# Weights-stationary product of a two-block transformer kernel: three 256-column matmuls a chunk in place of one of 512 and one of 256

## Chip, cores and metric

The kernel runs on one core of a Trainium2 chip. The metric is the device time of one execution in microseconds; lower is better. Three runs of the kernel before gave 3282.68, 3284.78 and 3285.42 us, so its time is the median, 3284.78 us.

## What is computed

Two transformer blocks over 256 tokens of 2048 features, all in float32. The lines that the change touches compute products of a weight matrix with the normed tokens, where the result is wanted with features on the partitions and tokens along the free axis:

```
proj = jnp.einsum('bsd,de->bse', h, w_in[l])            # block 1: q and k of two attentions
u = jax.nn.relu(jnp.einsum('bsd,df->bsf', h2, w_up[l])) # block 1: up projection, then u * u
proj = xn @ w_in[l]                                     # block 2: the mixers' projections
qry = jnp.einsum('td,dhk->thk', xt, w_query)            # block 2: PEER queries
hid = jax.nn.gelu(jnp.einsum('pd,phkd->phk', xb, u_tab[eb]), approximate=False)
y = jnp.einsum('phk,phkd->pd', gate * hid, v_tab[eb])
```

The last two lines are computed for all 16384 experts: `peer_u` holds them in 128 blocks of 128, and gates that are zero leave out the experts that were not chosen.

## The kernel before, in words

Every large product is made in two parts a factor: a float32 number is split into `hi` (rounded to float32r) and `lo` (the rest, also float32r), and of the four partial products the three largest are added up: hi·hi, hi·lo and lo·hi. The tokens are split once for each product stage into `XT`, two tiles of [128, 8, 2, 256], where the third axis is (hi, lo) and the last the 256 tokens. The weights come from HBM in pieces of [128, 2048], in two halves of [128, 1024] (`load`, L90), and each half is split as it arrives: ScalarE copies it to `hi` (L103), VectorE subtracts to give `lo` (L104).

There are two kinds of large product. In the first (`xpart`, L165 to L167, and `product`, L1184 to L1186) the tokens are stationary in TensorE and the weights move through in three matmuls of 512 columns. In the second, `wstat` (L117 to L130), the weights are stationary: for each of 16 chunks of 128 input features (8 to a half) the `hi` weights are loaded and all 512 columns of `XT` (hi and lo tokens) move through, into the full 512 columns of a PSUM bank (L125); then the `lo` weights are loaded and the 256 `hi` token columns move through, into the first half of that bank (L127). At the end the result is the sum of the two halves of the bank.

`wstat` is called 272 times, so 272 × 16 = 4352 pairs of matmuls: 64 times for the up projection (FFN), 128 times for `peer_u`, 16 times for the PEER queries and 64 times for the q, k and mixer projections (16 in each of `w1_qkf`, `w1_qka`, `w2_b`, `w2_fq`). Behind each call the two halves are added: ScalarE copies the second half to SBUF, VectorE adds the first half to it, and the rest of the work follows. These adds stand in `evac_w` (L285 and L286, then the scaling of L287), in the FFN (L516 and L517, then relu and square in L518), in the PEER queries (L1101 and L1102) and in the `peer_u` loop (L1151 and L1152, then the gelu in L1154 and L1156).

The order of the work on each engine is that of the program, with the split of the weights and the reading of results ahead (`tc.high_priority`), and a scheduler places the instructions of small background generators (attention, delta rule, HGRN2, top-k) between the large matmuls; `tick` moves them on after every half piece. In the `peer_u` loop the gate squares (`gates`, L1117) put two or four matmuls of 256 columns with their own stationary tiles between two `wstat` blocks. PSUM has four banks for results (`acc`) and four for small work (`misc`).

Of the kernel before, what the change touches and what calls it, by code (L numbers as in the profile page):

```python
# [21 lines left out]
OP = mybir.AluOpType  # L22
# [14 lines left out]
def build(tc, I, out):  # L37
# [27 lines left out]
    # ---- background work: generators that go on by a step after every half piece of weights, so that  # L65
# [42 lines left out]
    def split_to(hi, lo, src, scale=None):  # L108
        """hi, lo: float32r halves of src (times a per-partition scale)."""
        if scale is None:  # L110
            ins = S.activation(hi, src, AF.Copy)
            V.tensor_tensor(out=lo, in0=src, in1=hi.bitcast(F32), op=OP.subtract)  # L112
        else:
            ins = S.activation(hi, src, AF.Copy, scale=scale)
            V.scalar_tensor_tensor(lo, src, scale, hi.bitcast(F32), op0=OP.mult, op1=OP.subtract)  # L115
        return ins

    def wstat(src, X):
        """[128 features, 256 tokens] = W^T X; the two halves of the result's columns add up."""
        ps = acc()  # L120
        for s, (hi, lo) in enumerate(split(src)):
            for j in range(8):
                w = slice(j * 128, (j + 1) * 128)
                x = X[s][:, j]
                PE.matmul(ps, lhsT=hi[:, w], rhs=x.rearrange("p a t -> p (a t)"),  # L125
                          start=(s == 0 and j == 0), stop=False, skip_group_check=True)
                PE.matmul(ps[:, :T], lhsT=lo[:, w], rhs=x[:, 0], start=False,  # L127
                          stop=(s == 1 and j == 7), skip_group_check=True)
# [3 lines left out]
    def small_proj(name, n, X, r, pool, y, tag="evh"):  # L132
        """y [128 tokens, 2, n] = r * (X^T W) for a W of n columns, both of its parts stationary together"""
# [24 lines left out]
    def xpart(ps, part, X, k0, tt, first, last):  # L158
        """ps [128 tokens, 512 features] += X^T W over the two k-chunks of half a piece"""
# [9 lines left out]
    def xstat(srcs, X):  # L169
        """two banks [128 tokens, 512 features] = X^T W over the k-chunks of the pieces."""  # L170
# [9 lines left out]
    def out_proj(name, X, each):  # L180
        """X^T W in two k-halves of two feature blocks at a time: the second heads are needed late;
        each(nb, tt, ps) takes a result, and the very last pieces end with the first tokens first"""
# [25 lines left out]
    # matrix products that keep the tensor engine's clock up until the first data are there  # L208
# [36 lines left out]
    def rsqrt(dst, src, n, mul):  # L245
        """dst = (src * mul + eps) ** -0.5 for [128, n]"""
# [25 lines left out]
    def bcast(r, b, pool):  # L272
        """b [128, 256]: every partition holds r of the 256 tokens"""
# [7 lines left out]
    def evac_w(ps, dst, rB, pool):  # L281
        """dst = (first half + second half of the columns) * rB"""
        with tc.high_priority():
            t = pool.tile([128, T], F32, name="ev", bufs=3)
            ins = S.activation(t, ps[:, T:], AF.Copy)  # L285
            V.tensor_tensor(out=t, in0=ps[:, :T], in1=t, op=OP.add)  # L286
            V.tensor_tensor(out=dst, in0=t, in1=rB, op=OP.mult)  # L287
# [10 lines left out]
    def head_norm_t(o, dst, g, pool, h0, nh, z=None, ready=None):  # L298
        """dst[:, h] (hi, lo) = transpose of rmsnorm over the last axis of o[:, tt, h] (times z), times g"""
# [26 lines left out]
    # ================= block 1 =================  # L326
# [36 lines left out]
    # forgetting attention  # L363
# [81 lines left out]
    # stick-breaking attention  # L445
# [56 lines left out]
    # feed-forward in quarters of 2048 hidden features; the norm's scale is squared by relu^2  # L502
# [8 lines left out]
    def ffn_up(qr):  # L511
        hid[qr] = [act_tile(F32R), act_tile(F32R)]
        for f in range(16):
            ps = wstat(I["w1_up"][qr * 16 + f], XT)
            t = up.tile([128, T], F32, name="up_t", bufs=3)
            S.activation(t, ps[:, T:], AF.Copy)  # L516
            V.tensor_tensor(out=t, in0=ps[:, :T], in1=t, op=OP.add)  # L517
            V.scalar_tensor_tensor(t, t, 0.0, t, op0=OP.max, op1=OP.mult)  # L518
# [35 lines left out]
    # x = rmsnorm(x, g_final); the next norm's scale is that of x * g_final times both  # L554
# [12 lines left out]
    # ================= block 2: mixers =================  # L567
# [80 lines left out]
    def gdn_rest(j, ys):  # L648
        # l2 norms
# [14 lines left out]
        # beta * v, token layout  # L664
# [10 lines left out]
        # decays: L[t, s] and its transpose per tile, and from tile 0 to tile 1  # L675
# [50 lines left out]
        # Tm = (I - L)^-1 and its transpose U, by doubling  # L726
# [36 lines left out]
        # u = Tm (beta v - beta G u_prev), o = a u  # L763
# [128 lines left out]
    # four heads at a time, so that the activation tables of sigmoid, ln and exp change seldom  # L892
# [55 lines left out]
    # ================= block 2: PEER =================  # L948
# [27 lines left out]
    # queries, scores and the two rounds of top 16  # L976
# [30 lines left out]
    # A pair (i, j) of ranks can be among the 16 largest sums only if (i + 1) (j + 1) <= 16: all the pairs (i', j')  # L1007
    # with i' <= i and j' <= j come before it. So rows 0, 1 keep 16 columns, rows 2, 3 keep 8, rows 4..7 keep 4
    # and rows 8..15 keep one, in the order of the whole square.
    CANDS = ((0, 0, 2, 16), (32, 2, 2, 8), (48, 4, 4, 4), (64, 8, 8, 1))  # L1010

    def topk():
# [17 lines left out]
        # ranks of a pair: i the largest of p >> 4, (p >> 3) - 2, (p >> 2) - 8, p - 56, and j from the row's start  # L1030
# [19 lines left out]
        # gates  # L1050
# [9 lines left out]
        # chosen rows and columns of the expert square, slots on the partitions  # L1060
# [295 lines left out]
```

## Time and profile before

| what | value |
|---|---|
| median of three runs | 3284.78 us |
| lowest and highest run | 3282.68, 3285.42 us |
| span of the profiled execution | 3282.4 us |
| TensorE busy (PE) | 99% |
| weight loads busy (PEld) | 84% |
| VectorE, ScalarE busy | 67%, 52% |
| HBM traffic | 176 GB/s mean |

The page gives no time of the profiled execution apart from its span; the lowest run is 0.3 us above that span and the median 2.4 us. A matmul's recorded duration goes on past the start of the next matmul, because matmuls are pipelined, so the share of PE does not say how fast the columns go through; distances between starts do.

### The profile page before, as it was taken

Reading aid. Unit: us, or ns where it says so; the run is one execution under the profiler, and the core shown is the slowest. Engines: PE = TensorE matmul, PEld = TensorE weight load, DVE = VectorE, ACT = ScalarE, POOL = GpSimd, SP = SyncE. Lnnn points to the kernel's source line nnn. Section 1 sums busy time; section 2 is a strip of 40 time slices with the busy share of each in tenths; the row PEclk is TensorE's granted clock in tenths of the full one; section 3 lists DMA queues with packets and bytes.
Section 4 is the critical chain, followed back from the end, with each engine's and each line's share of the span. In section 5 each row is a group of like instructions: output and inputs, shape, how many; then the busy total and the mean of one; then the engine's idle time right before and its main releaser. Section 6 shows DMA issues by size and latency. Waiting matters only on the chain.

```text
span 3282.4 us, 45440 instructions
## 1 busy us (share of the span) xinstructions
PE 3254.2 (99%) x16980; PEld 2755.9 (84%) x16980; DVE 2191.2 (67%) x3659; ACT 1698.5 (52%) x2613; POOL 26.0 (1%) x40
## 2 busy tenths in 40 slices
PE   9999999999999999999999999999999999999998
PEld 7888888888888888888878888888888888888886
DVE  4556666555555686477669978888889655555554
ACT  5447554444443565555544456666555544444444
POOL 0000000000000000000000000000000000000000
PEclk9999999999999999999999999999999999999999
DMA  6454555555556543353455555555555655555654
GB/s 222 147 166 157 186 183 186 190 191 188 192 187 194 187 133 116 115 168 129 145 165 174 175 179 178 177 179 180 177 178 178 206 192 191 192 190 191 216 192 162
DMA packets 162415, 578.79 MB, mean 176 GB/s; under 512 B 19088, under 2 KB 20880, under 8 KB 161808
## 3 DMA queue, kind: packets, MB, share of 16 engines
q1 hardware_dynamic: 156384, 565.36, 52.6%
q10 hardware_dynamic: 5808, 10.52, 0.9%
q8 instruction: 133, 2.18, 0.3%
q14 instruction: 90, 0.74, 0.1%
HBM read 571.61 MB, written 4.19 MB: 175 GB/s over the span
## 4 chain that ended last, share of the span: by engine, by line
PE 92%; DVE 6%; ACT 1%; DMA 1%; issue 1%; POOL 0%; SPq 0%; DVEq 0%; POOLq 0%; ACTq 0%
PE acc L125 27%; PE acc L127 14%; PE acc L167 7%; PE acc L166 7%; PE acc L165 7%; PE acc L1186 7%; PE acc L1185 7%; PE acc L1184 7%; DVE lo L104 2%; PE misc L1117 1%; PE misc L873 1%; PE misc L758 1%; PE misc L750 1%; ACT hi L103 0%; PE misc L855 0%
## 5 line engine op out<-in xcount | busy, mean ns | idle before, releaser
L104 DVE TENSOR_TENSOR lo<-raw,hi 128x1024 fp32r<-128x1024 f32 x987 | 1206.6, 1223 | 867.5 <-ACT hi L103 523.4
L103 ACT ACTIVATE hi<-raw 128x1024 fp32r<-128x1024 f32 x1010 | 1070.4, 1060 | 1331.3 <-PE acc L166 368.6
L125 PE MATMUL acc<-xt,hi 128*128 128x512 f32 x4352 | 1554.8, 399 | 0.2 <-ACT hi L103 0.2
L127 PE MATMUL acc<-xt,lo 128*128 128x256 f32 x4168 | 1173.0, 281 | 1.4 <-DVE lo L104 1.3
L125 PEld LDWEIGHTS acc<-xt,hi 128*128 128x128 f32 x4352 | 819.2, 188 | 193.4 <-issue 2.3
L127 PEld LDWEIGHTS acc<-xt,lo 128*128 128x128 f32 x4168 | 782.9, 188 | 4.2 <-DVE lo L104 3.0
L1186 PE MATMUL acc<-lo,xt 128*128 128x512 f32 x1024 | 401.7, 393 | 1.2 <-DVE lo L104 1.2
L1185 PE MATMUL acc<-hi,xt 128*128 128x512 f32 x1024 | 401.7, 392 | 0.0
L1184 PE MATMUL acc<-hi,xt 128*128 128x512 f32 x1024 | 398.4, 389 | 0.0
L1184 PEld LDWEIGHTS acc<-hi,xt 128*128 128x128 f32 x1024 | 192.2, 188 | 43.6 <-DVE ut L1152 0.2
L1185 PEld LDWEIGHTS acc<-hi,xt 128*128 128x128 f32 x1024 | 192.3, 188 | 43.1 <-DVE xt L112 0.2
L1186 PEld LDWEIGHTS acc<-lo,xt 128*128 128x128 f32 x1024 | 192.3, 188 | 42.4 <-DVE lo L104 2.9
L167 PE MATMUL acc<-lo,act 128*128 128x512 f32 x512 | 199.5, 390 | 0.0
L166 PE MATMUL acc<-hi,act 128*128 128x512 f32 x512 | 199.5, 390 | 0.0
L165 PE MATMUL acc<-hi,act 128*128 128x512 f32 x512 | 199.2, 389 | 0.0
L165 PE MATMUL acc<-hi,xt 128*128 128x512 f32 x384 | 155.1, 405 | 3.3 <-ACT hi L103 3.2
L167 PE MATMUL acc<-lo,xt 128*128 128x512 f32 x384 | 152.0, 396 | 0.0
L166 PE MATMUL acc<-hi,xt 128*128 128x512 f32 x384 | 151.6, 395 | 0.4 <-DVE xt L115 0.4
L1114 DVE SCALAR_TENSOR_TENSOR oh<-c_iota,sl,slg 128x256 fp32r<-128x256 f32 x256 | 120.4, 477 | 0.0
L165 PEld LDWEIGHTS acc<-hi,act 128*128 128x128 f32 x512 | 96.1, 188 | 20.0
L167 PEld LDWEIGHTS acc<-lo,act 128*128 128x128 f32 x512 | 96.1, 188 | 19.9
L166 PEld LDWEIGHTS acc<-hi,act 128*128 128x128 f32 x512 | 96.1, 188 | 19.8
(579 smaller groups left out, 3064.8 us busy)
## 6 DMA issues: line engine op xcount, KB each, us to landing
raw<-in_peer_u SPq DMA_DIRECT2D x256, 512.0 KB, 3.9
raw<-in_peer_v SPq DMA_DIRECT2D x194, 512.0 KB, 4.5
raw<-in_w_up SPq DMA_DIRECT2D x128, 512.0 KB, 4.2
raw<-in_w_down SPq DMA_DIRECT2D x128, 512.0 KB, 4.5
raw<-in_w_qkf SPq DMA_DIRECT2D x32, 512.0 KB, 3.7
raw<-in_w_qka SPq DMA_DIRECT2D x32, 512.0 KB, 3.8
raw<-in_w_b SPq DMA_DIRECT2D x32, 512.0 KB, 3.8
raw<-in_w_fq SPq DMA_DIRECT2D x32, 512.0 KB, 3.8
```

Of the source, the lines that this page charges most:

```text
L103: S.activation(hi, r, AF.Copy)
L104: V.tensor_tensor(out=lo, in0=r, in1=hi.bitcast(F32), op=OP.subtract)
L125: PE.matmul(ps, lhsT=hi[:, w], rhs=x.rearrange("p a t -> p (a t)"), start=(s == 0 and j == 0), stop=False, skip_group_check=True)
L127: PE.matmul(ps[:, :T], lhsT=lo[:, w], rhs=x[:, 0], start=False, stop=(s == 1 and j == 7), skip_group_check=True)
L165: PE.matmul(ps, lhsT=x[:, 0], rhs=hi[:, w], start=(first and j == 0), stop=False)
L166: PE.matmul(ps, lhsT=x[:, 1], rhs=hi[:, w], start=False, stop=False)
L167: PE.matmul(ps, lhsT=x[:, 0], rhs=lo[:, w], start=False, stop=(last and j == 1))
L750: PE.matmul(wps[:, c * 128:(c + 1) * 128], lhsT=L[:, c], rhs=U[:, c], start=(c == 0), stop=True, skip_group_check=True)
L1114: V.scalar_tensor_tensor(oh2, iota[:, None].to_broadcast([128, 2, 128]), sl2[:, t:t + 1], slg.bitcast(F32)[:, t, :, None].to_broadcast([12 ...
L1184: PE.matmul(o, lhsT=x[:, 0], rhs=hi[:, w], start=first, stop=False)
L1185: PE.matmul(o, lhsT=x[:, 1], rhs=hi[:, w], start=False, stop=False)
L1186: PE.matmul(o, lhsT=x[:, 0], rhs=lo[:, w], start=False, stop=last)
```

## The change

`wstat` now uses only the first 256 columns of its bank. For each chunk it issues three matmuls of 256 columns, all accumulating into the same columns: hi weights with hi tokens, hi weights with lo tokens, lo weights with hi tokens. The result needs no add of halves, and the code behind each call reads it from PSUM directly.

```diff
-        ps = acc()
+        ps = acc()[:, :T]
         for s, (hi, lo) in enumerate(split(src)):
             for j in range(8):
                 w = slice(j * 128, (j + 1) * 128)
-                x = X[s][:, j]
-                PE.matmul(ps, lhsT=hi[:, w], rhs=x.rearrange("p a t -> p (a t)"),
-                          start=(s == 0 and j == 0), stop=False, skip_group_check=True)
-                PE.matmul(ps[:, :T], lhsT=lo[:, w], rhs=x[:, 0], start=False,
-                          stop=(s == 1 and j == 7), skip_group_check=True)
+                for a, b in ((hi, 0), (hi, 1), (lo, 0)):
+                    PE.matmul(ps, lhsT=a[:, w], rhs=X[s][:, j, b], start=(s == 0 and j == 0 and a is hi and b == 0),
+                              stop=(s == 1 and j == 7 and a is lo))
...
     def evac_w(ps, dst, rB, pool):
         with tc.high_priority():
-            t = pool.tile([128, T], F32, name="ev", bufs=3)
-            ins = S.activation(t, ps[:, T:], AF.Copy)
-            V.tensor_tensor(out=t, in0=ps[:, :T], in1=t, op=OP.add)
-            V.tensor_tensor(out=dst, in0=t, in1=rB, op=OP.mult)
+            ins = V.tensor_tensor(out=dst, in0=ps, in1=rB, op=OP.mult)
...
             t = up.tile([128, T], F32, name="up_t", bufs=3)
-            S.activation(t, ps[:, T:], AF.Copy)
-            V.tensor_tensor(out=t, in0=ps[:, :T], in1=t, op=OP.add)
-            V.scalar_tensor_tensor(t, t, 0.0, t, op0=OP.max, op1=OP.mult)
+            S.activation(t, ps, AF.Relu)
+            V.tensor_tensor(out=t, in0=ps, in1=t, op=OP.mult)
...
-            S.activation(qT, ps[:, T:], AF.Copy)
-            V.tensor_tensor(out=qT, in0=ps[:, :T], in1=qT, op=OP.add)
+            S.activation(qT, ps, AF.Copy)
...
-            t = pp2.tile([128, T], F32, name="ut", bufs=2)
-            S.activation(t, ps[:, T:], AF.Copy)
-            V.tensor_tensor(out=t, in0=ps[:, :T], in1=t, op=OP.add)
-            if n:
-                S.activation(t[:, :n], t[:, :n], AF.Gelu)
             if n < T:
-                S.activation(hb[:, n:], t[:, n:], AF.Gelu)
+                S.activation(hb[:, n:], ps[:, n:], AF.Gelu)
             if n:
+                t = pp2.tile([128, T], F32, name="ut", bufs=2)
+                S.activation(t[:, :n], ps[:, :n], AF.Gelu)
                 V.tensor_tensor(out=hb[:, :n], in0=t[:, :n], in1=hb[:, :n], op=OP.mult)
```

TensorE, at the first head of the delta rule in block 2, between the end of one `w2_b` block and the next. `gl`, `hn_sq` and `cv` are small tiles of the delta rule's gates, squares and convolved channels. Before:

```order
L125 MATMUL acc<-xt,hi 128x512
L127 MATMUL acc<-xt,lo 128x256
L618 MATMUL misc<-gl,c_le 128x16
L620 MATMUL misc<-gl,c_lst 128x8
L624 MATMUL misc<-c_le,gl 8x128 x2
L659 MATMUL misc<-ones,hn_sq 128x128 x2
L125 MATMUL acc<-xt,hi 128x512
L127 MATMUL acc<-xt,lo 128x256
L669 MATMUL misc<-ident,cv 128x128 x2
L125 MATMUL acc<-xt,hi 128x512
L669 MATMUL misc<-ident,cv 128x128 x2
L659 MATMUL misc<-ones,hn_sq 128x128 x2
```

The same place in the changed kernel (its lines 612, 614, 618, 653 and 663 are 618, 620, 624, 659 and 669 of the kernel before):

```order
L612 MATMUL misc<-gl,c_le 128x16
L614 MATMUL misc<-gl,c_lst 128x8
L618 MATMUL misc<-c_le,gl 8x128 x2
L125 MATMUL acc<-xt,hi 128x256
L125 MATMUL acc<-xt,lo 128x256
L125 MATMUL acc<-xt,hi 128x256 x2
L125 MATMUL acc<-xt,lo 128x256
...
L125 MATMUL acc<-xt,lo 128x256
L653 MATMUL misc<-ones,hn_sq 128x128 x4
L663 MATMUL misc<-ident,cv 128x128 x4
```

Where the pair of L125 and L127 stood, the changed kernel has two matmuls of the `hi` weights and one of the `lo` weights, all of 256 columns. The four sums of squares and four transposes, which stood in pieces between large matmuls, now stand in one run behind more of them; such runs of small matmuls are moved against the large ones at several places of the delta rule and of HGRN2, and nowhere else on TensorE.

VectorE in the `peer_u` loop, one block with its gates, before:

```order
L104 TENSOR_TENSOR lo<-raw,hi 128x1024 x2
L1109 TENSOR_TENSOR oh_18212<-c_iota,sl_14557 128x256
L1152 TENSOR_TENSOR ut<-acc,ut 128x256
L1124 TENSOR_TENSOR ut<-misc,ut 128x256
L1158 TENSOR_TENSOR H_14554<-ut,H_14554 128x48
L1114 SCALAR_TENSOR_TENSOR oh_18214<-c_iota,sl_14558,slg 128x256
L1125 TENSOR_TENSOR H_14554<-ut,H_14554 128x2x39
L1114 SCALAR_TENSOR_TENSOR oh_18217<-c_iota,sl_14558,slg 128x256
```

and one such block in the changed kernel (lines 1102, 1107, 1117, 1118 and 1148 answer to 1109, 1114, 1124, 1125 and 1158):

```order
L104 TENSOR_TENSOR lo<-raw,hi 128x1024 x2
L1102 TENSOR_TENSOR oh_21681<-c_iota,sl_16349 128x256
L1148 TENSOR_TENSOR H_16346<-ut,H_16346 128x72
L1117 TENSOR_TENSOR ut<-misc,ut 128x256
L1107 SCALAR_TENSOR_TENSOR oh_21683<-c_iota,sl_16350,slg 128x256
L1118 TENSOR_TENSOR H_16346<-ut,H_16346 128x2x49
L1107 SCALAR_TENSOR_TENSOR oh_21686<-c_iota,sl_16350,slg 128x256
```

The add of halves (L1152) is gone; the rest keeps its order but for the product with the gates, which now stands ahead of the next gate square's add. On ScalarE three more activation-table loads stand in the delta rule and HGRN2 than before (51 in place of 48).

## Rows read from the trace of the kernel before

**Rows 1.** The page, part 1: busy time, share of span and instructions of each engine.

```profile
PE 3254.2 (99%) x16980; PEld 2755.9 (84%) x16980; DVE 2191.2 (67%) x3659; ACT 1698.5 (52%) x2613; POOL 26.0 (1%) x40
```

**Rows 2.** The page, part 2: tenths of 40 slices of the span.

```profile
PE   9999999999999999999999999999999999999998
...
PEclk9999999999999999999999999999999999999999
```

**Rows 3.** The page, part 4: the chain that ended last, by engine.

```profile
PE 92%; DVE 6%; ACT 1%; DMA 1%; issue 1%; POOL 0%; SPq 0%; DVEq 0%; POOLq 0%; ACTq 0%
```

**Rows 4.** One line's instructions, L516, from 430 to 525 us: one each block.

```profile
L516 ACT ACTIVATE up_t<-acc x16: 366/366/367, 435.4 to 520.2; 128x256 f32<-128x256 f32 x16
```

**Rows 5.** Groups by line and form, 435 to 527 us (busy, mean ns, idle before).

```profile
L125 PE MATMUL acc<-xt,hi 128*128 128x512 f32 x262 | 92.6, 397 | 0.0
L127 PE MATMUL acc<-xt,lo 128*128 128x256 f32 x261 | 73.3, 281 | 0.0
L125 PEld LDWEIGHTS acc<-xt,hi 128*128 128x128 f32 x261 | 49.1, 188 | 12.1
L127 PEld LDWEIGHTS acc<-xt,lo 128*128 128x128 f32 x261 | 49.0, 188 | 0.0
```

**Rows 6.** Groups by line and form, 2002.76 to 2003.05 us: a run of two.

```profile
L1117 PE MATMUL misc<-oh,oh 128*128 128x256 f32 x2 | 0.4, 280 | 0.0
L1117 PEld LDWEIGHTS misc<-oh,oh 128*128 128x128 f32 x2 | 0.3, 188 | 0.0
...
L125 PEld LDWEIGHTS acc<-xt,hi 128*128 128x128 f32 x1 | 0.2, 188 | 0.0
```

**Rows 7.** L1117 from 1949 to 1950 us, a run of four: ns minimum/median/maximum.

```profile
L1117 PEld LDWEIGHTS misc<-oh,oh x4: 187/188/192, 1949.4 to 1949.7; 128*128 128x128 f32 x4
L1117 PE MATMUL misc<-oh,oh x4: 280/282/283, 1949.5 to 1949.8; 128*128 128x256 f32 x4
```

**Rows 8.** Groups by line and form, 1949.36 to 1949.90 us: the load behind the four.

```profile
L125 PEld LDWEIGHTS acc<-xt,hi 128*128 128x128 f32 x1 | 0.2, 192 | 0.0
```

**Rows 9.** Lines with their loads and matmuls: ns minimum/median/maximum, all occurrences.

```profile
L1117 PE MATMUL misc<-oh,oh x256: 278/280/385, 1916.8 to 2553.9; 128*128 128x256 f32 x128
L758 PEld LDWEIGHTS misc<-W,Tm x192: 186/192/192, 1207.5 to 1390.8; 128*128 128x128 f32 x192
L758 PE MATMUL misc<-W,Tm x192: 270/275/377, 1207.5 to 1390.9; 128*128 128x128 f32 x192
```

**Rows 10.** Timeline, 1240.5 to 1243 us: sixteen loads and matmuls of 128 columns.

```profile
1240.64 1.87 PEld L758 LDWEIGHTS misc<-W,Tm 128*128 128x128 f32 x16
1240.76 1.95 PE L758 MATMUL misc<-W,Tm 128*128 128x128 f32 x16
```

**Rows 11.** Groups by line: reading a result, and table loads.

```profile
L286 DVE TENSOR_TENSOR ev<-acc,ev 128x256 f32<-128x256 f32 x64 | 26.6, 418 | 2.0 <-ACT ev L285 2.0
L285 ACT ACTIVATE ev<-acc 128x256 f32<-128x256 f32 x64 | 23.4, 368 | 0.7 <-PE acc L127 0.6
L642 ACT ACT_TABLE_LOAD x5 | 6.4, 1283 | 0.1
```

**Rows 12.** Stretches: busy us (instructions) of PE, PEld, DVE, ACT, POOL; clock, DMA.

```profile
435.00:970.00 535.00, 535.00 (x2806) 457.39 (x2805) 316.38 (x400) 240.09 (x320) 0.00 (x0) 1.00 0.58 189
...
1150.00:1460.00 310.00, 306.95 (x1838) 264.48 (x1837) 203.31 (x390) 174.78 (x273) 10.61 (x21) 1.00 0.41 133
1460.00:1700.00 240.00, 237.56 (x1272) 201.44 (x1270) 171.40 (x295) 120.10 (x176) 3.82 (x3) 1.00 0.45 147
1700.00:1890.00 190.00, 185.18 (x1049) 159.49 (x1050) 175.55 (x594) 92.05 (x133) 0.55 (x1) 0.97 0.51 169
```

**Rows 13.** Waits of PEld: line, waited for, us in total, times, longest.

```profile
PEld acc L127 <- DVE lo L104: 3.0, 5, 1.0
...
PEld acc L125 <- ACT hi L103: 0.6, 1, 0.6
```

More of the change, by code (lines that the diff above doesn't have):

```diff
@@ L1149, in build @@
         with tc.high_priority():
-            t = pp2.tile([128, T], F32, name="ut", bufs=2)
-            S.activation(t, ps[:, T:], AF.Copy)
-            V.tensor_tensor(out=t, in0=ps[:, :T], in1=t, op=OP.add)
+            if n < T:
+                S.activation(hb[:, n:], ps[:, n:], AF.Gelu)
             if n:
-                S.activation(t[:, :n], t[:, :n], AF.Gelu)
-            if n < T:
-                S.activation(hb[:, n:], t[:, n:], AF.Gelu)
-            if n:
+                t = pp2.tile([128, T], F32, name="ut", bufs=2)
+                S.activation(t[:, :n], ps[:, :n], AF.Gelu)
                 V.tensor_tensor(out=hb[:, :n], in0=t[:, :n], in1=hb[:, :n], op=OP.mult)
```

## The prediction

> **What bounds the kernel now.** I read the engines' busy times first, then the slices, the chain, and the starts of matmuls in one steady stretch. TensorE is busy 99% of the span, its loads of weights 84%, VectorE 67%, ScalarE 52% [rows 1]; in 39 of 40 slices TensorE is at nine tenths or more, and the granted clock is full throughout [rows 2], the 2.4 GHz level. The chain that ended last lies 92% on TensorE [rows 3]. So a step off TensorE counts only where TensorE waits for it, and the question is how fast columns and weights go through TensorE, before and after.
>
> The FFN's up projection shows this without other work: each block ends with one L516, and sixteen of them start between 435.4 and 520.2 us [rows 4]. Fifteen blocks in 84.8 us are 5.653 us a block, and a block is 16 pairs: **353.3 ns a pair**. Recorded durations go on past the next matmul's start: 397 and 281 ns [rows 5] add to 678, so each overhangs by (678 - 353.3) / 2 = 162.3 ns. Taken off, the 512-column matmul holds TensorE 234.7 ns and the 256-column one 118.7 ns (the means are rounded: within 0.5). This is how I turn durations into distances below.
>
> **The change part by part.**
>
> *Three matmuls for two.* 4352 pairs become triples. Each chunk needs the same 768 columns, but three loads in place of two. What a 256-column matmul with a load of its own costs inside a sequence of such is shown in the `peer_u` loop only, where gate squares (L1117) follow an L127.
>
> - In a run of two the mean is 280 ns, the loads 188, and the load after them 188 [rows 6]: 280 - 162.3 = 117.7 ns apart. Three would make 353, what the pair costs.
> - In a run of four the durations go from 280 to 283 and the loads from 188 to 192 [rows 7], and the load behind the four also took 192 [rows 8]. Since two of the four are like the run of two and the median is 282, the last two lie at 282 to 283: 120 to 121 ns apart.
>
> So the first ones are cheap because a 512-column matmul ahead of them left time in which loads could run ahead; after about three that is used up and each costs some 2.5 ns more. The 128-column matmuls show the same end state: their loads have a median of 192 ns against a minimum of 186, and their durations 275 against 270 [rows 9]; sixteen in a row, 1.95 us long, are (1.95 - 0.275) / 15 = 112 ns apart [rows 10], whereas the shortest, 270 - 162.3, is 108. In the changed loop no 512-column matmul is left to catch up in, so I take the end state, 120 ns: a triple is 360 ns, 6.7 more than the pair, and 4352 × 6.7 = **+29.2 us**. The bounds: 278, the shortest L1117 [rows 9], gives 115.7 ns, 347 a triple and -27 us; 283 throughout gives 120.7, 362 and +38 us. I take 120 because only the run of four has more than three such matmuls in a row.
>
> The Trainium skill (TensorE: Matmul & The Clock Gate, Back-to-back issue gap) gives 262 cycles for 256 columns and 518 for 512. By it a pair is 780 cycles at 2.4 GHz, 325 ns, and a triple 786, 327.5; the sum would be 2.5 × 4352 = +11 us. The trace's pair is 28 ns longer than that, so its own runs decide here.
>
> *The adds of halves.* 272 results lose a VectorE add of 418 ns [rows 11], 114 us in all; 192 of them, those of `evac_w` and of `peer_u`, also lose a ScalarE copy of 368 ns [rows 11], 71 us (the PEER queries keep the copy, the FFN's becomes the relu). TensorE hides all of it where it is at 100%: from 435 to 970 us it is busy 535.0 of 535 us [rows 12]. Where it is not, 1700 to 1890 us, VectorE is at 175.6 of 190 and TensorE idles 4.8 us [rows 12]; `lo` coming late costs the loads of L127 3.0 us in five places, `hi` L125 0.6 [rows 13]. With 418 ns less VectorE work a block I give back 2 of these: **-2 us**, bounds 0 and -4.8.
>
> *What is moved.* In the delta rule and HGRN2 runs of small matmuls stand elsewhere. TensorE idles 3.0 us from 1150 to 1460 and 2.4 from 1460 to 1700 [rows 12], and a moved run can lose or win about that: 0, bounds -5.4 and +5.4. Three more table loads of 1.28 us [rows 11] fall on ScalarE, busy 175 of 310 us there [rows 12]: nothing, 3.9 us at most if none is covered. The shorter path behind a result, by an add and a copy, frees its bank 0.8 us earlier; a block takes 5.65 us and there are four banks, so nothing waits for one. DMAs, SP and their order stay the same.
>
> Sum: +29.2 - 2 = +27.2 on a span of 3282.4, 3309.6 us. The median of the runs lies 2.4 above that span, which I carry over: **3312 us**.
>
> **The rivals.**
>
> *Same pace.* The triple keeps a pace between the two kinds of row, 117.7 (run of two) and 118.7 (the L127 of the loop itself, whose moving data are those of the new matmuls): 354 to 356 ns, +3 to +11 us, less 2. For it: the L127 are by far the most numerous. Against it: each of them stands right behind a 512-column matmul. I take 118.3: +7 - 2, 3290 us.
>
> *Faster: a stall of the 512-column matmul goes.* Its 234.7 ns here are longer than two times the shortest 256-column distance, 2 × 115.7, so something in the alternation costs time, and a uniform stream might lose it: 117 ns each, 351 a triple, -10 us, less 2: 3273 us. Against it: the run of four gets slower, not faster, as it goes on. This ends on the other side, and decides if the distances hold at or under 117.5 from the fourth on.
>
> *The second load of the same weights is dropped*, since the first two matmuls of a triple share them. In the trace every matmul has its load (16980 each [rows 1]). Without it the middle matmul could save the load's share, from 120 down to the 112 that the loads alone need [rows 10]: 352 a triple, -6 - 2, 3277 us; in the faster rival's pace 3250.
>
> *Loads that do not overlap.* At 188 ns a load [rows 5], 4352 more would make 2755.9 + 818 = 3574 us of load time, more than the span. If each had to end before the next began, the kernel could not end before 3574. Against it: sixteen loads of 192 ns, 3.07 us, were done in 1.87 [rows 10], and four L1117 kept 120 ns. The Trainium skill states (TensorE: Matmul & The Clock Gate, The mechanism) that loads overlap with running matmuls only when their row groups differ; by that the 818 us would come on top, 4100. The trace disagrees: loads of full 128-row tiles run beside matmuls everywhere.
>
> **How the numbers follow.** End state of the run of four 0.40; same pace 0.25; faster stream 0.24; dropped load 0.07; loads that do not overlap, or another loss over 45 us, 0.04. The likeliest gives 3312, with its own range of 119 to 121 ns and the moved work, 3298 to 3322. A measurement of this kernel tells about 0.2%, 6.6 us, from no change. Of the same pace, two thirds (0.17) stay within that and a third (0.08) is slower; of the faster stream 0.15 is faster and 0.09 within; the dropped load is faster. So faster 0.22, same 0.26, slower 0.52. The range goes from the faster rival's 3272 to the upper end of the likeliest, 3322, and leaves out some 0.15.
>
> **What would show it.** In the FFN the sixteen reads of results (now a relu) would start 5.76 us apart, not 5.65; durations of L125 would be 282 to 283 with loads of 192; VectorE's busy time down by about 110 us, ScalarE's by some 70, weight loads 13056 in the loop, their busy share unchanged or less where records overlap. Distances of 117 or 118 with loads of 188 would show the first two rivals right; 4352 fewer loads than matmuls the third. TensorE waiting in the delta rule by more than 5 us longer than before would make the sum wrong in its zeros.

## The result and the profile after

The changed kernel takes **3251.0 us** (four runs, 3249.5 to 3251.2) where the kernel before takes 3285.1 (four runs beside it): ratio 0.9895, 95% interval 0.9883 to 0.9906. It is 1.05% or 34 us faster; forecast were 3312 us, and "slower" as the likeliest. The profiled execution took 3251.2 us and spans 3249.4, 33.0 less than before.

The page of the changed kernel: busy times by engine, the chain that ended last by engine, and the groups of the changed loop, all now on L125 (count, busy us, mean ns, idle before).

```profile
PE 3215.1 (99%) x21332; PEld 2920.2 (90%) x21332; DVE 2103.7 (65%) x3387; ACT 1645.7 (51%) x2424; POOL 25.2 (1%) x40
...
PE 95%; DVE 3%; DMA 1%; issue 0%; ACT 0%; POOL 0%; SPq 0%; DVEq 0%; POOLq 0%; ACTq 0%
...
L125 PE MATMUL acc<-xt,hi 128*128 128x256 f32 x8704 | 1519.0, 279 | 0.2 <-ACT hi L103 0.2
L125 PEld LDWEIGHTS acc<-xt,hi 128*128 128x128 f32 x8704 | 1319.4, 188 | 4.9 <-issue 3.2
L125 PE MATMUL acc<-xt,lo 128*128 128x256 f32 x4168 | 1157.3, 278 | 3.6 <-DVE lo L104 3.4
L125 PEld LDWEIGHTS acc<-xt,lo 128*128 128x128 f32 x4168 | 785.2, 188 | 5.0 <-DVE lo L104 4.8
```

Against [rows 1, 3]: 4352 more matmuls, each with its load (21332 of both); VectorE 87 us less busy, ScalarE 53 us; the chain lies still more on TensorE, 95% for 92%. So TensorE bounds as before, and what changed is its pace. The means of 279 and 278 are no duration that is common: they mix two. Groups by line and form, 435 to 527 us, the stretch of [rows 5], in the FFN's first quarter:

```profile
L125 PE MATMUL acc<-xt,hi 128*128 128x256 f32 x543 | 92.4, 276 | 0.0
L125 PEld LDWEIGHTS acc<-xt,hi 128*128 128x128 f32 x542 | 81.5, 188 | 0.0
L125 PE MATMUL acc<-xt,lo 128*128 128x256 f32 x271 | 74.8, 276 | 0.0
L125 PEld LDWEIGHTS acc<-xt,lo 128*128 128x128 f32 x271 | 50.9, 188 | 0.0
```

and the same groups from 700 to 790 us, in its third quarter:

```profile
L125 PE MATMUL acc<-xt,hi 128*128 128x256 f32 x418 | 73.9, 281 | 0.0
L125 PEld LDWEIGHTS acc<-xt,hi 128*128 128x128 f32 x417 | 63.7, 188 | 0.0
L125 PE MATMUL acc<-xt,lo 128*128 128x256 f32 x210 | 59.0, 281 | 0.0
L125 PEld LDWEIGHTS acc<-xt,lo 128*128 128x128 f32 x209 | 40.1, 192 | 0.0
```

The same code on the same shapes takes 276 ns a matmul in one place and 281 in the other, and in the second every third load takes 192 ns. The reads of results (L511, one a block) give the paces: one line's instructions (minimum/median/maximum ns, first and last start), from 430 to 525 and from 689 to 775 us.

```profile
L511 ACT ACTIVATE up_t<-acc x17: 364/365/366, 434.1 to 521.1; 128x256 f32<-128x256 f32 x17
...
L511 ACT ACTIVATE up_t<-acc x16: 363/364/367, 689.9 to 774.8; 128x256 f32<-128x256 f32 x16
```

Sixteen blocks in 87.0 us are 5.438 us a block, **340 ns a triple**, 113.3 a matmul; fifteen in 84.9 are 5.66, **some 353 ns a triple**, the pace of the pair before (84.8 us for fifteen, [rows 4]), 117.8 a matmul. I call them the fast and the slow rhythm; in the FFN durations of 276 mark the one, of 281 the other. The timeline of TensorE from 450 us shows the fast one: the starts of the matmuls with `lo` are 0.34 us apart.

```profile
449.88 0.28 PE L125 MATMUL acc<-xt,lo 128*128 128x256 f32 x1
449.99 0.39 PE L125 MATMUL acc<-xt,hi 128*128 128x256 f32 x2
450.22 0.28 PE L125 MATMUL acc<-xt,lo 128*128 128x256 f32 x1
```

Where the 33 us came from is read by landmarks: first and last start of lines that both kernels share. Of the kernel before (L165 the first matmul of the activations-stationary products, L1184 that of the last product):

```profile
L165 PE MATMUL acc<-hi,act x512: 387/389/398, 609.6 to 1141.4; 128*128 128x512 f32 x171
L165 PE MATMUL acc<-hi,xt x384: 387/392/794, 9.8 to 1697.8; 128*128 128x512 f32 x192
...
L1184 PE MATMUL acc<-hi,xt x1024: 388/388/467, 2565.3 to 3269.0; 128*128 128x512 f32 x171
```

The last product has three lines, whose recorded durations differ (groups by line and form, whole run):

```profile
L1185 PE MATMUL acc<-hi,xt 128*128 128x512 f32 x1024 | 401.7, 392 | 0.0
L1186 PE MATMUL acc<-lo,xt 128*128 128x512 f32 x1024 | 401.7, 393 | 1.2 <-DVE lo L104 1.2
L1184 PE MATMUL acc<-hi,xt 128*128 128x512 f32 x1024 | 398.4, 389 | 0.0
```

The landmarks of the changed kernel (L163, L1174 and, for the gate squares, L1110 are those lines):

```profile
L511 ACT ACTIVATE up_t<-acc x64: 363/365/367, 428.7 to 952.3; 128x256 f32<-128x256 f32 x64
...
L163 PE MATMUL acc<-hi,act x512: 387/389/394, 596.2 to 1127.8; 128*128 128x512 f32 x171
L163 PE MATMUL acc<-hi,xt x384: 387/394/793, 9.9 to 1685.5; 128*128 128x512 f32 x192
...
L1110 PE MATMUL misc<-oh,oh x256: 281/282/358, 1902.6 to 2521.1; 128*128 128x256 f32 x128
...
L1174 PE MATMUL acc<-hi,xt x1024: 387/392/397, 2532.1 to 3236.0; 128*128 128x512 f32 x171
```

The median of L1174 is 392 where that of L1184 was 388, but the product is no slower: the shortest of the three has moved to the third line (L1176, 389 from 2600 to 3200 us), and the 1024 take 704 us in both kernels. One line's duration does not give a stream's pace; those of all its lines do.

| landmark | before, us | after, us | ahead by | won since |
|---|---|---|---|---|
| first read of an FFN block [rows 4] | 435.4 | 428.7 | 6.7 | 6.7 |
| first down projection (after two quarters) | 609.6 | 596.2 | 13.4 | 6.7 |
| last FFN matmul of that line (quarters 3 and 4 between) | 1141.4 | 1127.8 | 13.6 | 0.2 |
| last product of the mixers (delta rule and HGRN2 between) | 1697.8 | 1685.5 | 12.3 | -1.3 |
| first gate square [rows 9] | 1916.8 | 1902.6 | 14.2 | 1.9 |
| first matmul of the last product (`peer_u` between) | 2565.3 | 2532.1 | 33.2 | 19.0 |
| end of span | 3282.4 | 3249.4 | 33.0 | -0.2 |

Quarters 1 and 2 are 512 triples at 340.0 for 353.3 ns: 6.8 us, what the second line shows. Quarters 3 and 4 run in the slow rhythm and win nothing, though they too have lost their adds. If all 4352 triples were fast the gain would be 58 us; the 33 us won are 57% of that (a share of the time, not a count of fast triples).

The mixers lost 1.3 us. Stretches of the changed kernel that answer to the last three of [rows 12], each 13.4 us earlier:

```profile
1136.60:1446.60 310.00, 304.35 (x2177) 278.77 (x2176) 195.41 (x367) 170.56 (x251) 9.77 (x21) 1.00 0.40 132
1446.60:1686.60 240.00, 237.29 (x1419) 207.99 (x1417) 168.74 (x282) 121.59 (x169) 3.82 (x3) 1.00 0.44 147
1686.60:1876.60 190.00, 182.60 (x1528) 179.50 (x1529) 168.52 (x569) 88.96 (x121) 0.55 (x1) 0.97 0.52 172
```

TensorE idles 5.7, 2.7 and 7.4 us there, before 3.0, 2.4 and 4.8. A faster TensorE, and small matmuls that stand elsewhere, wait 5.5 us more; which of the two it is was not tried.

### The profile page after: what moved, and what is told of

Its sections match the earlier page's. It is cut to its first block, busy times and chain, and to the rows that moved or that the text cites. A ratio compares the mean times of both kernels' runs of the same rounds, so it can differ in the third digit from the quotient of the medians.

```text
span 3249.4 us, 53531 instructions
## 1 busy us (share of the span) xinstructions
PE 3215.1 (99%) x21332; PEld 2920.2 (90%) x21332; DVE 2103.7 (65%) x3387; ACT 1645.7 (51%) x2424; POOL 25.2 (1%) x40
## 4 chain that ended last, share of the span: by engine, by line
PE 95%; DVE 3%; DMA 1%; issue 0%; ACT 0%; POOL 0%; SPq 0%; DVEq 0%; POOLq 0%; ACTq 0%
PE acc L125 44%; PE acc L163 8%; PE acc L165 8%; PE acc L164 8%; PE acc L1174 7%; PE acc L1175 7%; PE acc L1176 7%; PE misc L1110 1%; DVE lo L104 1%; PE misc L867 1%; PE misc L752 1%; PE misc L744 1%; PE misc L849 0%; PE misc L259 0%; DVE oh L1059 0%
## 5 line engine op out<-in xcount | busy, mean ns | idle before, releaser
L125 PE MATMUL acc<-xt,hi 128*128 128x256 f32 x8704 | 1519.0, 279 | 0.2 <-ACT hi L103 0.2
L125 PEld LDWEIGHTS acc<-xt,hi 128*128 128x128 f32 x8704 | 1319.4, 188 | 4.9 <-issue 3.2
L125 PE MATMUL acc<-xt,lo 128*128 128x256 f32 x4168 | 1157.3, 278 | 3.6 <-DVE lo L104 3.4
L125 PEld LDWEIGHTS acc<-xt,lo 128*128 128x128 f32 x4168 | 785.2, 188 | 5.0 <-DVE lo L104 4.8
L1174 PE MATMUL acc<-hi,xt 128*128 128x512 f32 x1024 | 401.8, 393 | 0.0
L1176 PE MATMUL acc<-lo,xt 128*128 128x512 f32 x1024 | 398.6, 390 | 1.0 <-DVE lo L104 1.0
L1176 PEld LDWEIGHTS acc<-lo,xt 128*128 128x128 f32 x1024 | 192.1, 188 | 46.4 <-DVE lo L104 3.1
L1174 PEld LDWEIGHTS acc<-hi,xt 128*128 128x128 f32 x1024 | 192.2, 188 | 42.9
L165 PE MATMUL acc<-lo,act 128*128 128x512 f32 x512 | 199.5, 390 | 0.0
L163 PE MATMUL acc<-hi,act 128*128 128x512 f32 x512 | 199.2, 389 | 0.0
L163 PE MATMUL acc<-hi,xt 128*128 128x512 f32 x384 | 155.8, 407 | 3.3 <-ACT hi L103 3.2
L165 PE MATMUL acc<-lo,xt 128*128 128x512 f32 x384 | 151.2, 394 | 0.0
L165 PEld LDWEIGHTS acc<-lo,act 128*128 128x128 f32 x512 | 96.1, 188 | 20.0
L163 PEld LDWEIGHTS acc<-hi,act 128*128 128x128 f32 x512 | 96.1, 188 | 19.5
```

Source lines behind the costliest of these rows:

```text
L125: PE.matmul(ps, lhsT=a[:, w], rhs=X[s][:, j, b], start=(s == 0 and j == 0 and a is hi and b == 0), stop=(s == 1 and j == 7 and a is lo))
L163: PE.matmul(ps, lhsT=x[:, 0], rhs=hi[:, w], start=(first and j == 0), stop=False)
L165: PE.matmul(ps, lhsT=x[:, 0], rhs=lo[:, w], start=False, stop=(last and j == 1))
L1174: PE.matmul(o, lhsT=x[:, 0], rhs=hi[:, w], start=first, stop=False)
L1176: PE.matmul(o, lhsT=x[:, 0], rhs=lo[:, w], start=False, stop=last)
```

## The experiments

Times are medians; each is compared with runs of the kernel before on the same chip. Where one run is noted there is no interval, and the reading rests on the durations. Rows are of the groups by line and form unless said otherwise. The labels in brackets are those by which later expectations name earlier experiments.

**The shape of the matmuls alone.** (e1) The kernel before, with the pair cut into three 256-column matmuls into the two halves of its bank; copies and adds of halves stay.

```diff
-                PE.matmul(ps, lhsT=hi[:, w], rhs=x.rearrange("p a t -> p (a t)"), ...
-                PE.matmul(ps[:, :T], lhsT=lo[:, w], rhs=x[:, 0], ...
+                for i, (a, c, o) in enumerate(((hi, 0, 0), (hi, 1, T), (lo, 0, 0))):
+                    PE.matmul(ps[:, o:o + T], lhsT=a[:, w], rhs=x[:, c], ...
```

> Three matmuls of 256 columns a chunk, but hi weights with lo tokens go into the second half of the bank and the adds of halves stay, as before. Theory P (the gain is TensorE's pace: a uniform stream of 256-column matmuls runs at 113.3 ns each where it is caught in the fast rhythm, 117.8 in the slow one): 3245 to 3275 us, FFN durations of L125 276 or 281 and nothing between. Rival R (the gain comes from the removed adds and copies): 3283 to 3288 us. Rival A (it comes from accumulating in one region): 3283 to 3288 us.

Measured 3253.6 us, ratio 0.9909 (0.9892 to 0.9925). In quarters 1 and 3 (435 to 527 and 700 to 790 us):

```profile
L126 PE MATMUL acc<-xt,hi 128*128 128x256 f32 x543 | 92.4, 276 | 0.0
...
L126 PE MATMUL acc<-xt,hi 128*128 128x256 f32 x422 | 74.6, 281 | 0.0
...
L126 PEld LDWEIGHTS acc<-xt,lo 128*128 128x128 f32 x211 | 40.5, 192 | 0.0
```

The same two rhythms in the same quarters, and 30 of the 34 us. The two intervals overlap, so the 2.6 us between this and the change are not clear of the noise.

**The removed adds alone.** (e2) The changed kernel's reads with the pair of before; the product of `hi` weights with `lo` tokens is left out of the result.

```diff
-                for a, b in ((hi, 0), (hi, 1), (lo, 0)):
-                    PE.matmul(ps, lhsT=a[:, w], rhs=X[s][:, j, b], ...
+                PE.matmul(ps, lhsT=hi[:, w], rhs=x.rearrange("p a t -> p (a t)"), ...
+                PE.matmul(ps[:, :T], lhsT=lo[:, w], rhs=x[:, 0], ...
...
-        return ps
+        return ps[:, :T]
```

> The pair of 512 and 256 columns as before, but every result is read as in the changed kernel, from the first half of the bank alone; the product of hi weights with lo tokens is computed and left out of the result. Theory P: 3281 to 3287 us, no change, with 353.3 ns a pair. Rival R: 3250 to 3256 us.

Measured 3283.0 us, ratio 1.0002 (0.9992 to 1.0011). VectorE is 87 us and ScalarE 51 us less busy than before, the pair as it was, from 435 to 527 us:

```profile
L125 PE MATMUL acc<-xt,hi 128*128 128x512 f32 x261 | 92.3, 397 | 0.0
L127 PE MATMUL acc<-xt,lo 128*128 128x256 f32 x262 | 73.6, 281 | 0.0
```

Leaving out the adds of halves is worth nothing that can be measured beside the pair, and beside the triples the 2.6 us of e1 are within the noise; the gain is in the form of the matmuls.

**Is it that two neighbours share their weights?** (e3) The changed kernel in the order hi, lo, hi:

```diff
-                for a, b in ((hi, 0), (hi, 1), (lo, 0)):
+                for a, b in ((hi, 0), (lo, 0), (hi, 1)):
```

> The changed kernel with the three matmuls in the order hi weights with hi tokens, lo weights, hi weights with lo tokens, so that no two loads in a row within a chunk take the same weights. Theory P: the two rhythms of 113.3 and 117.8 ns stay, the time lies between 3225 (fast throughout) and 3285 us (slow throughout), likely 3235 to 3265. Rival S (a second load of the same weights is cheaper): 117.8 ns throughout, 3282 to 3288 us.

Measured 3250.4 us, ratio 0.9900 (0.9884 to 0.9917). No neighbours share weights within a triple now, and nothing is lost. In the slow quarter (700 to 790 us) the longer load has gone from `lo` to one of the two `hi`: 190 is the mean of 188 and 192.

```profile
L125 PEld LDWEIGHTS acc<-xt,hi 128*128 128x128 f32 x420 | 64.5, 190 | 0.0
...
L125 PEld LDWEIGHTS acc<-xt,lo 128*128 128x128 f32 x210 | 39.4, 188 | 0.0
```

**Two matmuls of one width, 512.** (e4) The kernel before with `lo` times `lo` added, a third more columns:

```diff
-                PE.matmul(ps, lhsT=hi[:, w], rhs=x.rearrange("p a t -> p (a t)"), ...
-                PE.matmul(ps[:, :T], lhsT=lo[:, w], rhs=x[:, 0], ...
+                for a in (hi, lo):
+                    PE.matmul(ps, lhsT=a[:, w], rhs=x.rearrange("p a t -> p (a t)"), ...
```

> The kernel before with both matmuls of a pair 512 columns wide (lo weights with lo tokens is added to the result). It asks whether unequal widths hold the pair in the slow rhythm. If equal widths reach the fast rhythm: 226.7 ns each, 453.3 a pair, 4352 x 100 ns more, about 3720 us. If every 512-column matmul of this loop costs 235.6: 471 a pair, about 3797 us.

Measured 3770.9 us (one run), between the two. One line's instructions, 480 to 580 us:

```profile
L126 PE MATMUL acc<-xt,hi x206: 392/393/483, 483.0 to 579.7; 128*128 128x512 f32 x103
...
L126 PE MATMUL acc<-xt,lo x206: 392/398/475, 483.7 to 579.9; 128*128 128x512 f32 x103
```

These stay above the 389 of the down projection's 512-column matmuls (L165 above; L166 and L167 are 389 as well from 615 to 680 us). In quarter 3 of this kernel both lines are at 394. Equal widths are thus not all it takes.

**Small interruptions in the stream.** (e5) The changed kernel with one to four small matmuls into a bank that nobody reads, ahead of twelve blocks of the FFN.

```diff
+KICKS = {(0, 4): ("f32", 1), (0, 8): ("f32", 2), (0, 12): (128, 1), (1, 0): (512, 1), ...
...
+            if s == 0 and kick is not None:
...
+                    if kind == "f32":
+                        PE.matmul(kp_[:, :128], lhsT=ident, rhs=ident, start=True, stop=True)
+                    else:
+                        PE.matmul(kp_[:, :kind], lhsT=hi[:, :128], ...
...
-            ps = wstat(I["w1_up"][qr * 16 + f], XT)
+            ps = wstat(I["w1_up"][qr * 16 + f], XT, KICKS.get((qr, f)))
```

> The changed kernel with twelve small interruptions in the up projection, each one to four matmuls into a bank that nobody reads, at the start of a block: one, two or four of 128 columns with the float32 identity, one or two of 128 columns, or one of 512 columns. Theory E (the rhythm is caught at the entry of an undisturbed stream and held until something else comes between): after some of the interruptions the stream goes on in the other rhythm and stays in it until the next one; in the third and fourth quarter, slow throughout in the changed kernel, at least one stretch of four blocks runs at 113.3 ns, and in the first and second at least one may fall to 117.8. Rival F (the place decides: buffers, transfers, other engines): a few matmuls near each interruption differ, and the third and fourth quarter stay at 117.8 throughout. Time by E within 10 us of the changed kernel, by F 1 to 4 us over it.

Measured 3255.0 us (one run). The trace records every float32 matmul of an interruption as two, so "f32 x1" below is two records. Behind the interruption at 444 us, in a quarter that was fast, and behind the next at 467 us (447 to 466 and 470 to 488 us):

```profile
L138 PE MATMUL acc<-xt,hi 128*128 128x256 f32 x109 | 19.4, 281 | 0.0
...
L138 PE MATMUL acc<-xt,hi 128*128 128x256 f32 x108 | 18.4, 276 | 0.0
```

Each stretch between two interruptions is in one rhythm from end to end. After the twelve it was, in order, by the durations of L138 between one and the next (kind and number, rhythm after):

| quarter | rhythm at its start | first | second | third |
|---|---|---|---|---|
| 1 | fast | f32 x1: slow | f32 x2: fast | 128 x1: slow |
| 2 | slow | 512 x1: slow | f32 x4: fast | 128 x2: fast |
| 3 | slow | f32 x1: fast | f32 x2: fast | 128 x1: slow |
| 4 | slow | 512 x1: fast | f32 x4: fast | 128 x2: fast |

(Quarter 2 follows quarter 1 without a break, and goes on in its rhythm; its first interruption stands at its first block.) So a rhythm is caught when a stream begins or goes on after something else, and held; no stretch of the FFN is bound to one rhythm. What comes out at the start of a quarter is not random, however: in the nine traces with triples in the FFN (the change, e1, e3, e5, e7 and e9 to e12) quarter 1 begins at 276 and quarter 3 at 281.

**The last product cut to 256 columns.** (e7) The changed kernel, six matmuls for three of 512:

```diff
-        PE.matmul(o, lhsT=x[:, 0], rhs=hi[:, w], start=first, stop=False)
...
+        for i, (b, part) in enumerate(((0, hi), (1, hi), (0, lo))):
+            for c in range(2):
+                PE.matmul(o[:, c * 256:(c + 1) * 256], lhsT=x[:, b], ...
...
```

> The changed kernel with the last product (tokens stationary, weights moving in three matmuls of 512 columns) cut the same way: six matmuls of 256 columns, every stationary tile loaded twice. Before, the three take 686 ns. In the fast rhythm six take 680: 1024 x -6.7 = -7 us, 3244 us; in the slow one 706.7: +21 us, 3272 us. Theory P expects 113.3 or 117.8 ns and nothing between; a rival by which every further load costs something of its own expects more than 118 ns and over 3275 us.

Measured 3272.1 us, six runs from 3250.4 to 3273.1, ratio 0.9951 (0.9928 to 0.9975). In the profiled run of 3258.2 us, from 2600 to 3000 and from 3060 to 3240 us:

```profile
L1176 PE MATMUL acc<-hi,xt 128*128 128x256 f32 x2353 | 362.5, 276 | 0.0
...
L1176 PE MATMUL acc<-hi,xt 128*128 128x256 f32 x1023 | 161.4, 279 | 0.0
```

The product left the fast rhythm on its way, and the trace shows where: behind the only wait of the loads between the two stretches, for weights whose transfer ScalarE had waited 5.0 us for (waits of PEld, 3000 to 3065 us: in all, times, longest).

```profile
PEld acc L1176 <- DVE lo L104: 3.1, 1, 3.1
```

After it the granted clock is 0.53 from 3036.5 to 3040 us, about the 1.2 GHz level, and 0.98 from 3040 to 3044; from there on the durations are 279 and 280. Six matmuls start 0.71 us apart there, 706.7 ns by the slow pace of the FFN: so the slow rhythm has a recorded duration of 279 here and of 281 there, and here its loads take 188 ns. Three of 512 took 688 (704 us from the first to the last of 1024 L1174). The cut product thus wins 8 ns or loses 19 for each three, and the spread of the runs fits executions that fall into the slow rhythm at different times; only one of them has a trace.

**Two matmuls of one width, 384.** (e8) The pair of the second experiment, cut evenly:

```diff
-                x = X[s][:, j]
-                PE.matmul(ps, lhsT=hi[:, w], rhs=x.rearrange("p a t -> p (a t)"), ...
-                PE.matmul(ps[:, :T], lhsT=lo[:, w], rhs=x[:, 0], ...
+                x = X[s][:, j].rearrange("p a t -> p (a t)")[:, :384]
+                for a in (hi, lo):
+                    PE.matmul(ps[:, :384], lhsT=a[:, w], rhs=x, ...
```

> The pair of the kernel before, but with both matmuls 384 columns wide: the same 768 columns and two loads a chunk, equal widths. It leaves out the hi weights' product with the second 128 tokens beyond column 384 of the moving tile, and reads the first half of the result only, as e2 does. Theory 'unequal widths hold the slow rhythm': 384-column matmuls can run at 170 ns (3 x 113.3 / 2), 340 a pair, where they are caught fast, so the first two FFN quarters have 16 blocks in 87 us, and the kernel takes 3225 to 3260 us. Theory 'fewer, longer matmuls a chunk cost it': 353.3 a pair stays everywhere, 16 blocks in 90.5 us, and the kernel takes 3281 to 3287 us.

Measured 3266.1 us (one run), between the two theories' times. In quarters 1 and 3 (435 to 527 and 700 to 790 us):

```profile
L126 PE MATMUL acc<-xt,hi 128*128 128x384 f32 x267 | 89.6, 335 | 0.0
...
L126 PE MATMUL acc<-xt,lo 128*128 128x384 f32 x225 | 76.2, 339 | 0.0
```

Again two rhythms in the same two places, so two matmuls a chunk can leave the pace of the pair. The reads of quarter 1 (one line's instructions) give the fast one, 17 blocks in 94.4 us, 347 ns a chunk; three of 256 do it in 340.

```profile
L512 ACT ACTIVATE up_t<-acc x18: 363/364/367, 430.5 to 524.9; 128x256 f32<-128x256 f32 x18
```

**Interruptions to win back slow stretches.** (e9 to e11) Three kernels: the changed one with two float32 matmuls at the start of quarters 3 and 4 and of HGRN2's first projection; that and the same in the last product of 512 columns; that with the product cut to 256.

```diff
+    def kick():
+        k = misc()
+        for i in range(2):
+            PE.matmul(k[:, :128], lhsT=ident, rhs=ident, start=True, stop=True)
...
+            if f == 0 and qr >= 2:
+                kick()
```

> The changed kernel, and two float32 identity matmuls of 128 columns into a bank that nobody reads, at the start of the third and of the fourth FFN quarter and before the first HGRN2 projection. Theory 'the rhythm is caught at the entry and held': the two quarters, which ran at 353.3 ns a triple, are caught at 340: 2 x 16 blocks of 16 triples x 13.3 ns = 6.8 us, HGRN2 up to 1.3 us, against 3 interruptions of some 0.4 us: 3243 to 3247 us. Theory 'the place decides': 3251 to 3253 us.

> e9 and the same interruption ahead of every eighth group of the last product, whose matmuls are 512 columns wide, four in all. If a stream of 512-column matmuls has a fast rhythm too (680 ns for three instead of 686), the product loses up to 1%, 7 us against e9, less 1.5 us of interruptions. If it has only one pace, it is 1.5 us above e9.

> e9, with the last product cut into 256-column matmuls as in e7, and the interruption ahead of every fourth group, eight in all. If each interruption gives a new draw of the rhythm, a stretch that falls to 353.3 ns is won back at the next one: in the fast rhythm throughout it would be 680 for 686 ns, some 7 us under e9, less 3 us of interruptions; with half of the stretches slow it would be some 10 us above e9. If the place decides, it varies as e7 did, 3250 to 3273 us.

Measured 3251.7 (ratio 0.9903, 0.9886 to 0.9919), 3253.5 (0.9912, 0.9896 to 0.9929) and 3275.7 us (0.9980, 0.9970 to 0.9990), in this order. Of the first, quarter 3 (700 to 790 us), and of the third, the product (2600 to 3200 us):

```profile
L130 PE MATMUL acc<-xt,hi 128*128 128x256 f32 x421 | 74.5, 281 | 0.0
```

```profile
L1185 PE MATMUL acc<-hi,xt 128*128 128x256 f32 x3370 | 533.6, 279 | 0.0
```

The first came out as the theory "the place decides" had it (3251 to 3253), the second as its branch "only one pace" (1.8 us above the first, forecast 1.5); the third lies above both of its theories. An interruption ahead of a quarter did not change what it caught, and the product of 256 columns stayed slow behind all eight. The product of 512 columns kept the pace of before, though the down projection shows that 512 columns can go faster: 389 on all three lines, 680 ns for three. So an interruption is no free draw, and at the start of a quarter the theory of a catch at the entry is not told apart from the place.

**The interruption one block later.** (e12) The changed kernel with one small matmul at the second block of quarters 3 and 4; the code that issues it is that of e5.

```diff
+KICKS = {(2, 1): ("f32", 1), (3, 1): (512, 1)}
```

> The changed kernel with two small interruptions after the first block of a slow quarter, not ahead of it: one float32 matmul of 128 columns at block 1 of quarter 3, one of 512 columns at block 1 of quarter 4, the kinds that brought these quarters from 281 to 276 ns at block 4 in e5. Theory 'an interruption gives a new draw, and what is caught is held': if both draws are fast again, 30 blocks of 16 triples x 13.3 ns = 6.4 us less, interruptions 0.6 us more: 3244 to 3247 us; if one, 3248 to 3250; if none, 3251 to 3253. Theory 'the kind of interruption decides, wherever it stands': both fast, 3244 to 3247.

Measured 3245.6 us (3243.5 to 3247.0), ratio 0.9885 (0.9868 to 0.9901). Quarter 3 and quarter 4 (700 to 790 and 880 to 950 us):

```profile
L138 PE MATMUL acc<-xt,hi 128*128 128x256 f32 x420 | 71.4, 276 | 0.0
...
L138 PE MATMUL acc<-xt,hi 128*128 128x256 f32 x388 | 66.0, 276 | 0.0
```

Both quarters begin at 281 as before and are fast behind the interruption, the reads of each from its second block on 76.2 us for 14 blocks, 340 ns a triple:

```profile
L524 ACT ACTIVATE up_t<-acc x15: 363/365/368, 696.1 to 772.3; 128x256 f32<-128x256 f32 x15
...
L524 ACT ACTIVATE up_t<-acc x15: 365/365/366, 870.7 to 946.9; 128x256 f32<-128x256 f32 x15
```

This is the fastest kernel of the study. Its ratio alone does not set it apart from the change, since the intervals overlap; the durations do. Both theories had this time, so it does not tell them apart.

**The same twelve interruptions for the pair.** (e13) The kernel before with the edit of e5.

> The kernel before with the twelve interruptions of e5 in the FFN. Theory 'unequal widths hold the pair in the slow rhythm': after every one of the twelve the pair is at 353.3 ns again, 16 blocks in 90.5 us less the interruption, durations 397 and 281, and the kernel takes 3285 to 3289 us. Rival 'the pair was never caught well, but could be': after some of the twelve it runs at 340 to 347 ns a pair (durations of 390 and 275), as the triples did after seven of the twelve in e5, and the time is 3 to 10 us lower.

Measured 3288.2 us (one run). Medians over all four quarters (one line's instructions, 430 to 980 us):

```profile
L136 PE MATMUL acc<-xt,hi x1018: 388/397/482, 429.6 to 967.2; 128*128 128x512 f32 x170
...
L138 PE MATMUL acc<-xt,lo x1018: 279/281/284, 429.9 to 967.5; 128*128 128x256 f32 x170
```

The pair came back to 397 and 281, where triples were fast behind eight of the twelve (the expectation says seven, one too few). Between each two interruptions its medians are 397 and 281: it has only the slow rhythm here.

## Why the prediction was wrong

*The failed step is "Three for two", the +29.2 us.* It took 120 ns for a matmul of 256 columns, from the run of four gate squares [rows 7, 8]. Measured are 113.3 where the stream is fast and 117.8 where it is slow, 340.0 or 353.3 a triple; 360 stands nowhere for long. Four matmuls behind a pair show how TensorE gets from one rhythm into another, not where a long stream settles. The load of 192 ns, which I read as the sign of an end state in which catching up has stopped, is one load of three in the FFN's slow rhythm, which is no dearer than the pair.

*The bounds failed too.* The shortest L1117, 115.7 ns, was taken as the floor, but it too stood behind pairs. Nearer evidence was in the trace of before and in none of my rows: the down projection's 512-column matmuls have a median of 389 ns (L165 above), the pair's 397 [rows 5]. The same form is 8 ns longer in the pair, and the triples show another 5 (276 for 281): together the 13 ns a triple wins, 58 us if all did.

*The rival "a stall of the 512-column matmul goes"* (0.24) had the sign and the place; its reason, a uniform stream that loses what the alternation costs, fits the runs without being shown. Its 117 ns were mis-sized: 113.3 where the stream is fast, and 57% of what that would win throughout. Its test, 117.5 or less from the fourth on, was the right one. *Same pace* (0.25) is what the slow stretches do, without its 0.5 ns more. *Dropped load* and *loads that do not overlap* fall by the count of loads, and by loads of 188 ns that start 113 apart; that the dropped load's second figure, 3250, lies next to the 3251.0 measured is luck.

*By the skill's figures* (the Trainium skill, TensorE: Matmul & The Clock Gate, Back-to-back issue gap: 262 and 518 cycles) a triple costs 2.5 ns more than a pair. That section gives them as the gap of a single matmul in isolation, and here every matmul stands in a stream with a load of its own. The trace disagrees: 13.3 less or the same, and a matmul of 256 columns in these streams at 113.3 or 117.8 ns, not at 262 cycles' 109.

*The adds of halves, -2 us*: the experiment without them found nothing (ratio 1.0002). VectorE fell by 87 us and ScalarE by 53, not 110 and 70. The waits I meant to win back grew: L125 waits 4.8 us for `lo` [rows 13 had 3.0], as a faster TensorE that comes for it sooner would make them; this was not tried. *What is moved, 0*: 1.3 us lost in the mixers, within the bounds of 5.4. *What would show it*: reads 5.44 or 5.66 us apart instead of 5.76.

**What stays open.** Shown is that three equal matmuls of 256 columns and two of 384 can catch a fast rhythm and that the pair of 512 and 256 does not, under any entry tried. Not shown is why: two of 512 do not reach the down projection's pace, so equal widths are not enough by themselves. What in an entry decides is open as well. Interruptions of two or four matmuls (as the program counts them) within the FFN's stream were followed by the fast rhythm in six of six cases, but two ahead of the stream or in the product were not, and single ones went either way, four fast of eight. The wait of 3.1 us in the cut product shows that a pause can throw a stream into the slow rhythm.

## What to carry to other kernels

Price a new form of matmul by long streams, and compare the recorded duration of one form, over all its lines, in every stream of the trace: the same 512 columns at 389 ns here and 397 there said that the mixture lost time, and the even cut won part of it back, with half as many loads again. A run of three or four matmuls prices an entry, not a stream. After such a change look for stretches with two mean durations, and try a small matmul a block behind the start of a slow one; whether it helps has to be measured in each place, since the same thing ahead of the stream and in the last product won nothing.

## What the runs showed of the hardware

A stream of equal matmuls with a load each keeps one of two paces, and in the long stretches looked at nothing between: 113.3 or 117.8 ns for 256 columns, 347 or some 353 ns for two of 384 (recorded durations 335 or 339). At 256 columns the recorded duration is 276 in the fast rhythm, and in the slow one 281 in the FFN and 279 in the last product. Three of 512 columns take 680 ns in the down projection and 688 in the last product, before and after. In the changed kernel the granted clock is 1.00 from 421.6 to 1686.6 us, the 2.4 GHz level, so it does not tell the two apart, nor does any wait within a stretch; a load of 192 ns marks the slow rhythm in the FFN, but not in the product. One float32 matmul between two blocks, two records in the trace, changed the pace of the next 80 us (quarter 3 of e12). That 4352 more loads fit in beside the columns is also new to me. Loads of 188 ns start every 113 ns, so they overlap one another. Their recorded busy share rose from 84% to 90% of the span; within the FFN it is 100% in the fast stretch (92.0 of 92.0 us from 435) and in the slow one alike (80.0 of 80.0 from 870). So the share of PEld says little of how much room is left.
